# Gated SSD and S5 mixers on one Trainium2 core: scores and their products with the decays in PSUM, decay differences on ScalarE, y in one set of columns

## Chip, core and metric

The kernel runs on one core of a Trainium2 chip. The metric is the device time of one execution in microseconds. A core has TensorE (PE, matmuls; its weight loads are listed apart as PEld), VectorE (DVE), ScalarE (ACT), GpSimd (POOL) and SyncE (SP, which here issues transfers). Each engine works through its own list of instructions in order; a scheduler has fixed these lists when the kernel is built, and semaphores hold an engine back until what it needs is there.

## What is computed

One layer of a streaming encoder: 2048 positions and 16 learned meta tokens of width 1024, a gated SSD branch (16 heads of 64 in 4 groups, state 128) beside an S5 branch, and a squared-ReLU MLP. The change lies in the SSD branch alone. Its core in the reference:

```python
da_cs = jnp.cumsum(dt_c * a.reshape(g, r), axis=2)
seg = da_cs[:, :, :, None] - da_cs[:, :, None, :]
decay = jnp.exp(jnp.where(causal, seg, -jnp.inf))
scores = jnp.einsum("bclgn,bcsgn->bclsg", cc, bc)
y_diag = jnp.einsum("bclsg,bclsgr,bcsgrp->bclgrp", scores, decay, xdt)
states = jnp.einsum("bclgn,bclgr,bclgrp->bcgrpn", bc, decay_states, xdt)
...
y_off = jnp.einsum("bclgn,bcgrpn,bclgr->bclgrp", cc, h_prev, jnp.exp(da_cs))
return (y_diag + y_off).reshape(b, seq_len, n_heads, p)
```

The kernel takes chunks of 128 positions instead of 64, which gives the same function. So for each chunk and group of 4 heads there is one 128x128 matrix of scores, four 128x128 matrices of decays (one a head), their products, and y as the product of these with the inputs.

## The kernel before

The 2048 positions are worked through in four blocks (b = 0 to 3) of 512, each of four chunks (c) of 128. In a block, the groups g = 0 to 3 follow each other. For a group PE makes, as its main load, four units of the x/B/C projection (`xbc`, each followed by a convolution, `conv_tile`) and four units of the z and gate projection (`rhs_group`, evacuated by `evac_zg` at L1208 and L1209 into `zg`); each unit is 24 matmuls of 512 columns (in block 0, with the meta tokens, an `xbc` unit is 48 of 264). These matmuls write the banks `pd`, four in all, and a bank is free for the next unit when its evacuation has read it. Between the units `step()` puts the small work of the scan: with t counting the units of a group, t = 2 starts the decays (`Ssd.start`), t = 4 to 7 do `front(0)`, `front(1)`, `back(0)`, `front(2)`; `back(1)`, `front(3)`, `back(2)` and `back(3)` fall into t = 0 to 3 of the next group. The order in which an engine gets these instructions is the scheduler's, which shifts them further.

All matmul operands are split into a high and a low part, and `mm3` makes high x high, high x low and low x high, three matmuls into one result (L244, L245, L246).

What the change touches, for one chunk:

- `front(c)`: the inputs xs are transposed into the PSUM bank `sst` (L787) and scaled; `xhl` holds their high and low parts side by side. The scores go to the bank `psc` and are masked with the triangle `tri` into the SBUF tile `smask` (L837, VectorE). L839 multiplies the decays `csb` (SBUF, four heads) by it in place; ScalarE casts the result to its high part `mh` (L842), VectorE makes the low part `ml` (L843).
- `back(c)`: `pyo` is the part from the carried state, of which `hTh` (ScalarE, L811) and `hTl` are the parts. For each head L853 multiplies `mh` by both halves of `xhl` at once, 128 columns (high half and low half of the result stand side by side), and L855 adds `ml` times the high half on 64 columns. VectorE makes y from `pyo` (L861, four times) and adds both halves of `py` (L864, twice).
- `decays`: one DMA on SyncE's queue (L885) spreads the cumulated decays of a group over 128 partitions, 1 MB in SBUF (`csb`; one buffer in block 0, two in blocks 1 to 3). Then 16 VectorE instructions (L889, four chunks by four heads) subtract the column of cs and limit to zero, and one ScalarE instruction takes the exponential of all (L890).

Of the kernel before, what the change touches and what calls it, by code (L numbers as in the profile page):

```python
# [127 lines left out]
def _body(ctx, tc, d, out):  # L128
# [647 lines left out]
    class Ssd:  # L776
# [5 lines left out]

        def inputs(self, x, dts, i0, cs_, L):
            pl = self.pl
            pt = bank("sst")
            for i in range(2):
                T.transpose(pt[:L, i * P:(i + 1) * P], self.sd.xs[:, i, cs_], ident)  # L787
            x.pth = pt[:L, 0:256].rearrange("p (h q) -> p h q", h=4)
            x.xdt = pl.tile([P, 4, 64], F32, name="xdt", tag="xdt")
            xdd = pl.tile([P, 4, 64], F32, name="xdd", tag="xdd")  # L790
            V.tensor_tensor(x.xdt[:L], x.pth, h4(dts.dt, L, i0), op=ALU.mult)
            G.tensor_tensor(xdd[:L], x.xdt[:L], h4(dts.ds, L, i0), op=ALU.mult)
            x.xddh = pl.tile([P, 256], F32R, name="xddh", tag="xddh", bufs=2)
            x.xddl = pl.tile([P, 256], F32R, name="xddl", tag="xddl", bufs=2)
            xf = xdd.rearrange("p h q -> p (h q)")
            S.copy(x.xddh[:L], xf[:L])
            G.tensor_tensor(x.xddl[:L], xf[:L], x.xddh[:L].bitcast(F32), op=ALU.subtract)
# [14 lines left out]
            G.tensor_tensor(self.hl, f, self.hh.bitcast(F32), op=ALU.subtract)  # L812

        def start(self):
            self.dec = decays(self.pl, self.dts, self.g, self.b)

        def meta_in(self):
            self.mk = _K()
# [5 lines left out]
        def front(self, c):  # L824

            pl, sd, g, x = self.pl, self.sd, self.g, self.ck[c]
            x.cs_ = cs_ = slice(sd.t0 + c * P, sd.t0 + (c + 1) * P)
            self.inputs(x, self.dts, c * NH + g * 4, cs_, P)
            x.dx = pl.tile([P, 4, 64], F32, name="dx", tag="dx", bufs=2)
            V.tensor_tensor(x.dx, x.pth, drow[:, g * 4:g * 4 + 4].unsqueeze(2).broadcast_to([P, 4, 64]), op=ALU.mult)  # L830
            x.xhl = pl.tile([P, 4, 2, 64], F32R, name="xhl", tag="xhl", bufs=2)
            S.copy(x.xhl[:, :, 0, :], x.xdt)
            G.tensor_tensor(x.xhl[:, :, 1, :], x.xdt, x.xhl[:, :, 0, :].bitcast(F32), op=ALU.subtract)
            psc = bank("psc")
            mm3(psc[:, 0:P], sd.bh[:, cs_], sd.bl[:, cs_], sd.ch[:, cs_], sd.cl[:, cs_], True, True)
            sm = pl.tile([P, P], F32, name="smask", tag="smask", bufs=2)
            V.tensor_tensor(sm, psc[:, 0:P], tri, op=ALU.mult)  # L837
            csb = self.dec[:, c]
            V.tensor_tensor(csb, csb, sm.unsqueeze(1).broadcast_to([P, 4, P]), op=ALU.mult)  # L839
            x.mh = pl.tile([P, 4, P], F32R, name="mh", tag="mh", bufs=2)  # L840
            x.ml = pl.tile([P, 4, P], F32R, name="ml", tag="ml", bufs=2)
            S.copy(x.mh, csb)  # L842
            V.tensor_tensor(x.ml, csb, x.mh.bitcast(F32), op=ALU.subtract)  # L843

        def back(self, c):

            pl, sd, g, x, dts = self.pl, self.sd, self.g, self.ck[c], self.dts
            i0, cs_ = c * NH + g * 4, x.cs_
            py, po = bank("py"), bank("pyo")
            mm3(po[:, 0:256], sd.ch[:, cs_], sd.cl[:, cs_], self.hh, self.hl, True, True)  # L850
            pyv = py.rearrange("p (h a q) -> p h a q", h=4, a=2)
            for h in range(4):
                T.matmul(pyv[:, h].rearrange("p a q -> p (a q)"), x.mh[:, h, :],  # L853
                         x.xhl[:, h].rearrange("p a q -> p (a q)"), start=True, stop=False)
                T.matmul(pyv[:, h, 0, :], x.ml[:, h, :], x.xhl[:, h, 0, :], start=False, stop=True)  # L855
            self.update(x, sd.bth[:, c, :], sd.btl[:, c, :], dts.cd, i0, P)
            if c < NC4 - 1:
                self.split()
            x.y = y = pl.tile([P, 4, 64], F32, name="y_", tag="y_", bufs=2)
            for h in range(4):  # L860
                V.scalar_tensor_tensor(y[:, h, :], po[:, h * 64:h * 64 + 64], dts.E[:, i0 + h:i0 + h + 1],  # L861
                                       x.dx[:, h, :], op0=ALU.mult, op1=ALU.add)
            for a in range(2):
                V.tensor_tensor(y, y, pyv[:, :, a, :], op=ALU.add)  # L864

        def gate(self, c):

# [13 lines left out]
    def decays(pl, dts, g, b):  # L881

        t = pl.tile([P, NC4, 4, P], F32, name="csb", tag="csb", bufs=2 if b else 1)
        src = csd[b].rearrange("(c h) l -> c h l", h=NH)[:, g * 4:g * 4 + 4, :]
        nc.sync.dma_start(t, src.unsqueeze(0).broadcast_to([P, NC4, 4, P]))  # L885
        for c in range(NC4):
            for h in range(4):
                i = c * NH + g * 4 + h
                V.tensor_scalar(t[:, c, h, :], t[:, c, h, :], dts.cs[:, i:i + 1], 0.0, op0=ALU.subtract, op1=ALU.min)  # L889
        S.activation(t, t, AF.Exp)  # L890
        return t


    xp = pool("xn", stack=xp_st)
# [195 lines left out]
    for b in range(NB):  # L1090
# [22 lines left out]
        def step(mm):  # L1113

            n = step.n
            step.n += 1
            g, t = divmod(n, 8)
            with tc.issue_after(mm):
                if n == 0:
                    dts.turn()  # L1120
                    dts.sums()
                if g < NG:
                    x = ssd[g]
                    if t == 2:
                        x.start()
                    elif t == 4:
                        if b == 0:
                            x.meta_in()
                        x.front(0)
                    elif t == 5:  # L1130
                        if b == 0:
                            x.meta_out()
                        x.split()
                        x.front(1)
                    elif t == 6:
                        x.back(0)
                    elif t == 7:
                        x.front(2)
                        x.gate(0)
                if g > 0:  # L1140
                    x = ssd[g - 1]
                    if t == 0:
                        x.back(1)
                        x.gate(1)
                    elif t == 1:
                        x.front(3)
                    elif t == 2:
                        x.back(2)
                        x.gate(2)
                    elif t == 3:  # L1150
                        x.back(3)
                        x.gate(3)
                for f in later:
                    f()
                later.clear()
                if b == 0:
                    s5.step(n - 1)
                if n >= KSTART:
                    next(kept, None)
# [606 lines left out]
```

## Time and profile before

| | |
|---|---|
| median of 3 runs | 3305.94 us (3300.7 to 3306.1) |
| the profiled execution | 3306.5 us, its span 3304.8 us |
| mean granted clock of TensorE | 0.968 |
| busy: PE, DVE, POOL, ACT | 93%, 64%, 43%, 37% |
| mixers (blocks 0 to 3) | about 205 to 1860 us of the span |
| MLP | about 1860 to 3304 us |

The span runs from the first to the last instruction of the profiled execution; 1.7 us of its time lie around it. Times in rows are counted from the span's start. A row of idle time names the engine or transfer whose event ended the wait. Block 0 runs from about 205 to 730, block 1 to 1110, block 2 to 1465, block 3 to 1860; block 0 has the S5 scan of its own and its larger share of VectorE's work besides.

### The profile page before, as it was taken

The page shows a single profiled execution, that of the slowest core. Times are in us where ns is not written, and L with a number is a line of the kernel's source. Part 1 is how long each engine was busy: PE and PEld are TensorE (multiplying, and loading weights), DVE is VectorE, ACT ScalarE, POOL GpSimd, SP SyncE. Part 2 cuts the span into 40 slices and gives each one's busy share as a digit, 9 for nine tenths or more (in the row PEclk, how much of TensorE's full clock was granted, in tenths as well). Part 3 has the DMA queues.
Part 4 walks back from the last instruction along what each step waited for, and adds up shares of the span by engine and source line. Part 5 has one row for each costly group of instructions (what it writes and reads, how often), then busy time and mean ns, then how long its engine had stood idle before and what let it go on. Part 6 is the DMA issues. An engine that isn't in the chain of part 4 may idle for free. (4 is left out here: it accounts for less than half of the span.)

```text
span 3304.8 us, 50038 instructions
## 1 busy us (share of the span) xinstructions
PE 3083.7 (93%) x18353; PEld 2751.1 (83%) x18353; DVE 2105.5 (64%) x4298; ACT 1231.2 (37%) x2573; POOL 1428.1 (43%) x1736
## 2 busy tenths in 40 slices
PE   7899999998999999998999788998979999989998
PEld 6678888877888778876888688888979999989998
DVE  8969998426843576426854477767675555475555
ACT  6345554434432443334433343344442121142222
POOL 3346766523522344213433465665642222243443
PEclk9999999999999999999999889999989999999999
DMA  6477676775556654566756767777788888889998
GB/s 210 143 214 203 199 205 205 284 245 155 173 189 216 201 169 158 204 221 195 226 178 209 255 252 275 261 275 265 276 283 284 246 250 245 249 286 377 358 358 277
DMA packets 297877, 782.92 MB, mean 237 GB/s; under 512 B 90688, under 2 KB 132800, under 8 KB 268448
## 3 DMA queue, kind: packets, MB, share of 16 engines
q0 software_dynamic: 88832, 411.21, 37.4%
q1 hardware_dynamic: 206192, 367.29, 33.8%
q8 instruction: 146, 2.39, 0.3%
q10 hardware_dynamic: 2608, 1.22, 0.1%
q14 instruction: 99, 0.81, 0.1%
HBM read 563.66 MB, written 218.05 MB: 237 GB/s over the span
## 5 line engine op out<-in xcount | busy, mean ns | idle before, releaser
L1505 DVE TENSOR_TENSOR acc<-acc,p 128x512 f32<-128x512 f32 x330 | 225.7, 684 | 171.6 <-PE p L246 169.1
L244 PE MATMUL pd<-hnh,wc 128*128 128x384 f32 (+1 forms) x896 | 292.9, 328 | 34.9 <-DMA wc<-wcd 21.3
L244 PE MATMUL pd<-wu,xnh 128*128 128x512 f32 x768 | 309.8, 404 | 3.5 <-ACT cacc L750 3.0
L246 PE MATMUL pd<-wu,xnl 128*128 128x512 f32 x768 | 308.9, 402 | 0.0
L245 PE MATMUL pd<-wu,xnh 128*128 128x512 f32 x768 | 308.3, 401 | 0.0
L246 PE MATMUL pd<-hnh,wc 128*128 128x384 f32 (+1 forms) x896 | 291.6, 328 | 13.7 <-DVE wc L1346 10.5
L245 PE MATMUL pd<-hnl,wc 128*128 128x384 f32 (+1 forms) x896 | 291.8, 326 | 0.0
L228 POOL DMA_DIRECT2D wu<-wsd x168 | 96.0, 572 | 373.0 <-PE pd L246 305.6
L1356 POOL DMA_DIRECT2D wr<-wcd x227 | 122.3, 539 | 274.8 <-PE pd L246 138.7
L244 PE MATMUL pd<-xnh,wu 128*128 128x512 f32 (+1 forms) x640 | 232.8, 364 | 7.7 <-DMA wu<-wsd 6.5
L246 PE MATMUL pd<-xnh,wu 128*128 128x512 f32 (+1 forms) x640 | 229.3, 359 | 0.0
L245 PE MATMUL pd<-xnl,wu 128*128 128x512 f32 (+1 forms) x640 | 229.0, 358 | 0.0
L1356 POOL DMA_DIRECT2D wc<-wcd x221 | 118.3, 536 | 252.8 <-PE pd L246 136.8
L244 PEld LDWEIGHTS pd<-hnh,wc 128*128 128x128 f32 x896 | 173.6, 194 | 40.0 <-ACT hnh L994 13.5
L753 DVE SCALAR_TENSOR_TENSOR cacc<-craw,conv,cacc 128x512 f32<-128x512 f32 (+1 forms) x192 | 174.9, 912 | 24.5 <-ACT cacc L750 17.1
L246 PEld LDWEIGHTS pd<-hnh,wc 128*128 128x128 f32 x896 | 173.6, 194 | 19.9 <-DVE wc L1346 14.3
L244 PEld LDWEIGHTS pd<-wu,xnh 128*128 128x128 f32 x768 | 146.1, 190 | 35.4 <-ACT cacc L750 3.9
L245 PEld LDWEIGHTS pd<-hnl,wc 128*128 128x128 f32 x896 | 173.7, 194 | 0.0
L246 PEld LDWEIGHTS pd<-wu,xnl 128*128 128x128 f32 x768 | 146.3, 191 | 31.8 <-issue 0.2
L245 PEld LDWEIGHTS pd<-wu,xnh 128*128 128x128 f32 x768 | 146.0, 190 | 31.4 <-issue 0.2
L218 POOL TENSOR_TENSOR wu<-wst,wu 128x1024 fp32r<-128x1024 f32 x56 | 137.1, 2448 | 73.6 <-ACT wu L217 72.5
L244 PEld LDWEIGHTS pd<-xnh,wu 128*128 128x128 f32 x640 | 125.5, 196 | 24.9 <-issue 7.9
(1015 smaller groups left out, 9967.7 us busy)
## 6 DMA issues: line engine op xcount, KB each, us to landing
wu<-wsd POOLq DMA_DIRECT2D x168, 1024.0 KB, 5.3
wr<-wcd POOLq DMA_DIRECT2D x227, 512.0 KB, 5.1
wcd<-wc SPq DMA_DIRECT2D x224, 512.0 KB, 3.0
wc<-wcd POOLq DMA_DIRECT2D x221, 512.0 KB, 5.5
wsd<-wu SPq DMA_DIRECT2D x56, 1024.0 KB, 5.2
wst<-in_w SPq DMA_DIRECT2D x60, 512.0 KB, 5.8
csb<-csd SPq DMA_DIRECT2D x16, 1024.0 KB, 14.3
xt<-in_x SPq DMA_DIRECT2D x28, 512.0 KB, 3.8
```

The lines of the kernel that those rows point to most:

```text
L218: eng.tensor_tensor(t[:, 1], raw, t[:, 0].bitcast(F32), op=ALU.subtract)
L228: nc.gpsimd.dma_start(t, wsd[u - U_XBC])
L244: T.matmul(ps, lh, rh, start=first, stop=False, skip_group_check=open_)
L245: T.matmul(ps, lh, rl, start=False, stop=False, skip_group_check=open_)
L246: return T.matmul(ps, ll, rh, start=False, stop=last, skip_group_check=open_).ins
L753: V.scalar_tensor_tensor(acc[:, :n], raw[:, k:k + n], conv[:, mt, k:k + 1], acc[:, :n], op0=ALU.mult, op1=ALU.add)
L1356: nc.gpsimd.dma_start(t, wcd[di * 28 + j])
L1505: V.tensor_tensor(o, o, pv, op=ALU.add)
```

## The change

Three things are changed. First, the scores no longer have the bank `psc`: their matmuls write columns 256 to 383 of the bank `sst` that holds the transposed inputs, the mask is applied there in place, and the product with the decays is written to the bank `psc` instead of in place into `csb`; ScalarE's cast and VectorE's low part read it from there. Second, the differences in `decays` are made by ScalarE: 16 Relu instructions with scale -1 and cs as bias give the differences with the other sign, and the exponential takes scale -1. `decays` is now a generator in three pieces: the DMA is called at the end of t = 1, the first eight Relus in t = 2, the rest and the exponential in t = 3. Third, each head's y is made by `mm3` on one set of 64 columns, three matmuls instead of two, and VectorE adds `py` once.

```diff
@@ -782,7 +782,7 @@
 
         def inputs(self, x, dts, i0, cs_, L):
             pl = self.pl
-            pt = bank("sst")
+            x.pt = pt = bank("sst")
             for i in range(2):
                 T.transpose(pt[:L, i * P:(i + 1) * P], self.sd.xs[:, i, cs_], ident)
             x.pth = pt[:L, 0:256].rearrange("p (h q) -> p h q", h=4)
@@ -812,7 +812,8 @@
             G.tensor_tensor(self.hl, f, self.hh.bitcast(F32), op=ALU.subtract)
 
         def start(self):
-            self.dec = decays(self.pl, self.dts, self.g, self.b)
+            self.decs = decays(self.pl, self.dts, self.g, self.b)
+            self.dec = next(self.decs)
 
         def meta_in(self):
             self.mk = _K()
@@ -831,12 +832,11 @@
             x.xhl = pl.tile([P, 4, 2, 64], F32R, name="xhl", tag="xhl", bufs=2)
             S.copy(x.xhl[:, :, 0, :], x.xdt)
             G.tensor_tensor(x.xhl[:, :, 1, :], x.xdt, x.xhl[:, :, 0, :].bitcast(F32), op=ALU.subtract)
-            psc = bank("psc")
-            mm3(psc[:, 0:P], sd.bh[:, cs_], sd.bl[:, cs_], sd.ch[:, cs_], sd.cl[:, cs_], True, True)
-            sm = pl.tile([P, P], F32, name="smask", tag="smask", bufs=2)
-            V.tensor_tensor(sm, psc[:, 0:P], tri, op=ALU.mult)
-            csb = self.dec[:, c]
-            V.tensor_tensor(csb, csb, sm.unsqueeze(1).broadcast_to([P, 4, P]), op=ALU.mult)
+            sm = x.pt[:, 256:256 + P]
+            mm3(sm, sd.bh[:, cs_], sd.bl[:, cs_], sd.ch[:, cs_], sd.cl[:, cs_], True, True, True)
+            V.tensor_tensor(sm, sm, tri, op=ALU.mult)
+            csb = bank("psc").rearrange("p (h l) -> p h l", h=4)
+            V.tensor_tensor(csb, self.dec[:, c], sm.unsqueeze(1).broadcast_to([P, 4, P]), op=ALU.mult)
             x.mh = pl.tile([P, 4, P], F32R, name="mh", tag="mh", bufs=2)
             x.ml = pl.tile([P, 4, P], F32R, name="ml", tag="ml", bufs=2)
             S.copy(x.mh, csb)
@@ -848,11 +848,9 @@
             i0, cs_ = c * NH + g * 4, x.cs_
             py, po = bank("py"), bank("pyo")
             mm3(po[:, 0:256], sd.ch[:, cs_], sd.cl[:, cs_], self.hh, self.hl, True, True)
-            pyv = py.rearrange("p (h a q) -> p h a q", h=4, a=2)
+            pyv = py[:, 0:256].rearrange("p (h q) -> p h q", h=4)
             for h in range(4):
-                T.matmul(pyv[:, h].rearrange("p a q -> p (a q)"), x.mh[:, h, :],
-                         x.xhl[:, h].rearrange("p a q -> p (a q)"), start=True, stop=False)
-                T.matmul(pyv[:, h, 0, :], x.ml[:, h, :], x.xhl[:, h, 0, :], start=False, stop=True)
+                mm3(pyv[:, h], x.mh[:, h, :], x.ml[:, h, :], x.xhl[:, h, 0, :], x.xhl[:, h, 1, :], True, True)
             self.update(x, sd.bth[:, c, :], sd.btl[:, c, :], dts.cd, i0, P)
             if c < NC4 - 1:
                 self.split()
@@ -860,8 +858,7 @@
             for h in range(4):
                 V.scalar_tensor_tensor(y[:, h, :], po[:, h * 64:h * 64 + 64], dts.E[:, i0 + h:i0 + h + 1],
                                        x.dx[:, h, :], op0=ALU.mult, op1=ALU.add)
-            for a in range(2):
-                V.tensor_tensor(y, y, pyv[:, :, a, :], op=ALU.add)
+            V.tensor_tensor(y, y, pyv, op=ALU.add)
 
         def gate(self, c):
 
@@ -883,12 +880,15 @@
         t = pl.tile([P, NC4, 4, P], F32, name="csb", tag="csb", bufs=2 if b else 1)
         src = csd[b].rearrange("(c h) l -> c h l", h=NH)[:, g * 4:g * 4 + 4, :]
         nc.sync.dma_start(t, src.unsqueeze(0).broadcast_to([P, NC4, 4, P]))
+        yield t
         for c in range(NC4):
             for h in range(4):
                 i = c * NH + g * 4 + h
-                V.tensor_scalar(t[:, c, h, :], t[:, c, h, :], dts.cs[:, i:i + 1], 0.0, op0=ALU.subtract, op1=ALU.min)
-        S.activation(t, t, AF.Exp)
-        return t
+                S.activation(t[:, c, h, :], t[:, c, h, :], AF.Relu, bias=dts.cs[:, i:i + 1], scale=-1.0)
+            if c == 1:
+                yield
+        S.activation(t, t, AF.Exp, scale=-1.0)
+        yield
 
 
     xp = pool("xn", stack=xp_st)
@@ -1121,8 +1121,8 @@
                     dts.sums()
                 if g < NG:
                     x = ssd[g]
-                    if t == 2:
-                        x.start()
+                    if t in (2, 3):
+                        next(x.decs)
                     elif t == 4:
                         if b == 0:
                             x.meta_in()
@@ -1150,6 +1150,8 @@
                     elif t == 3:
                         x.back(3)
                         x.gate(3)
+                if t == 1 and g < NG:
+                    ssd[g].start()
                 for f in later:
                     f()
                 later.clear()
```

What the scheduler makes of it, at three places. First ScalarE in block 1, from the cast of group 0's last chunk (`mh`) to the first gate evacuation that follows the next exponential; `hTh` are the state casts of the two coming chunks, `csb_9047` and `csb_9050` are the decays of group 2. Before:

```order
L842 CAST mh_8437<-csb_7985 128x512 [waits DVE_49]
L811 CAST hTh_8518<-hT_101 128x256 [waits DVE_49,Activation_49]
L811 CAST hTh_8700<-hT_101 128x256 [waits PE_49,Activation_49]
L873 ACTIVATE dx_8269,yss_8530<-y__8522 128x256 [waits DVE_49]
L759 CAST ch_8298<-cacc_8565 128x512 [waits PE_49]
L890 ACT_TABLE_LOAD [waits DMAHW7_49,DVE_49]
L890 ACTIVATE csb_9047<-csb_9047 128x2048 [waits Activation_49]
L769 CAST bth_8300<-btp_8610 128x512 [waits PE_49]
L1208 ACT_TABLE_LOAD
L1208 ACTIVATE zg_8795<-pd_8617 128x256 [waits PE_49]
```

After:

```order
L842 CAST mh_8471<-psc_8469 128x512 [waits DVE_49,Activation_49]
L887 ACTIVATE csb_9050<-csb_9050,cs_7925 128x128 [waits DMAHW7_49]
L887 ACTIVATE csb_9050<-csb_9050,cs_7925 128x128 x15
L811 CAST hTh_8547<-hT_101 128x256 [waits DVE_49,Activation_49]
L811 CAST hTh_8739<-hT_101 128x256 [waits PE_49,Activation_49]
L870 ACTIVATE dx_8302,yss_8558<-y__8551 128x256 [waits DVE_49]
L749 COPY craw_9014<-pd_8989 128x512 [waits PE_49]
L890 ACT_TABLE_LOAD
L890 ACTIVATE csb_9050<-csb_9050 128x2048 [waits Activation_49]
L1210 ACT_TABLE_LOAD
L1210 ACTIVATE zg_8854<-pd_8659 128x256 [waits DVE_49]
```

The 16 Relus and their wait for the transfer (DMAHW) stand behind `mh` and ahead of both `hTh`; the evacuations of `zg` stand behind the exponential as before.

VectorE at the same place, before:

```order
L804 TENSOR_TENSOR hT_101<-hT_101,pS_8512 128x256 [waits PE_49]
L864 TENSOR_TENSOR y__8522<-y__8522,py_8499 128x256 [waits DVE_49] x2
L870 TENSOR_TENSOR y__8522<-y__8522,zg_8246 128x256 [waits DVE_49]
L874 TENSOR_SCALAR yss_8530<-yss_8530 128x1 [waits Activation_49]
L889 TENSOR_SCALAR csb_9047<-csb_9047,cs_7893 128x128 [waits DMAHW7_49]
L889 TENSOR_SCALAR csb_9047<-csb_9047,cs_7893 128x128 x15
L877 SCALAR_TENSOR_TENSOR y__8522<-y__8522,yrs_8533,nwssd_7820 128x256 [waits Pool_49]
L861 SCALAR_TENSOR_TENSOR y__8595<-pyo_8577,E_7894,dx_8425 128x64 [waits PE_49]
L861 SCALAR_TENSOR_TENSOR y__8595<-pyo_8577,E_7894,dx_8425 128x64 x3
```

After:

```order
L861 TENSOR_TENSOR y__8551<-y__8551,py_8524 128x256 [waits DVE_49,PE_49]
L804 TENSOR_TENSOR hT_101<-hT_101,pS_8541 128x256 [waits PE_49,Pool_49]
L867 TENSOR_TENSOR y__8551<-y__8551,zg_8279 128x256 [waits DVE_49]
L871 TENSOR_SCALAR yss_8558<-yss_8558 128x1 [waits Activation_49]
L874 SCALAR_TENSOR_TENSOR y__8551<-y__8551,yrs_8561,nwssd_7852 128x256 [waits Pool_49]
L875 SCALAR_TENSOR_TENSOR mixA_7832<-zg_8279,y__8551 128x256 [waits DVE_49]
L804 TENSOR_TENSOR hT_101<-hT_101,pS_8630 128x256 [waits PE_49]
L859 SCALAR_TENSOR_TENSOR y__8636<-pyo_8614,E_7926,dx_8460 128x64 [waits PE_49]
```

The 16 subtractions and their wait for the transfer are gone from this queue, and one addition of `py` (L864 before, L861 after) a chunk.

PE, the beginning of `back` for one chunk (group 0 of block 1, chunk 2): the part from the state and the y of two of the four heads. Before:

```order
L246 MATMUL pd_8619<-wu_8537,xnl_6989 128x512
L245 MATMUL pyo_8500<-hTl_8359,ch_7825 128x256 [waits Pool_49]
L246 MATMUL pyo_8500<-hTh_8358,cl_7826 128x256
L853 MATMUL py_8499<-xhl_8271,mh_8281 128x128 [waits DVE_49]
L855 MATMUL py_8499<-xhl_8271,ml_8282 128x64
L853 MATMUL py_8499<-xhl_8271,mh_8281 128x128
L855 MATMUL py_8499<-xhl_8271,ml_8282 128x64
```

After:

```order
L244 MATMUL pyo_8525<-hTh_8394,ch_7857 128x256 [waits PE_49]
L245 MATMUL pyo_8525<-hTl_8395,ch_7857 128x256 [waits Pool_49]
L246 MATMUL pyo_8525<-hTh_8394,cl_7858 128x256
L244 MATMUL py_8524<-xhl_8304,mh_8313 128x64 [waits PE_49]
L245 MATMUL py_8524<-xhl_8304,mh_8313 128x64
L246 MATMUL py_8524<-xhl_8304,ml_8314 128x64
L244 MATMUL py_8524<-xhl_8304,mh_8313 128x64
L245 MATMUL py_8524<-xhl_8304,mh_8313 128x64
L246 MATMUL py_8524<-xhl_8304,ml_8314 128x64
```

A head's two matmuls of 128 and 64 columns have become three of 64.

## Rows read from the trace of the kernel before

**Rows 1.** The page, busy us, share of the span and instructions of each engine.

```profile
PE 3083.7 (93%) x18353; PEld 2751.1 (83%) x18353; DVE 2105.5 (64%) x4298; ACT 1231.2 (37%) x2573; POOL 1428.1 (43%) x1736
```

**Rows 2.** Windows: stretch, us, PE, PEld, DVE, ACT, POOL busy, clock, DMA, GB/s.

```profile
205.00:490.00 285.00, 262.37 (x1635) 230.91 (x1636) 263.33 (x510) 147.12 (x327) 194.38 (x194) 0.94 0.73 206
490.00:730.00 240.00, 238.25 (x1168) 193.18 (x1167) 129.71 (x258) 106.06 (x211) 117.14 (x102) 1.00 0.71 241
...
1465.00:1860.00 395.00, 366.12 (x1789) 302.29 (x1788) 238.98 (x515) 161.69 (x310) 148.83 (x213) 0.97 0.62 203
```

**Rows 3.** VectorE's groups, 205 to 1860: form, count | busy, mean ns | idle before.

```profile
L839 DVE TENSOR_TENSOR csb<-csb,smask 128x512 f32<-128x512 f32 x64 | 75.4, 1184 | 1.1
L843 DVE TENSOR_TENSOR ml<-csb,mh 128x512 fp32r<-128x512 f32 x64 | 61.1, 959 | 14.4 <-ACT mh L842 14.3
L889 DVE TENSOR_SCALAR csb<-csb,cs 128x128 f32<-128x128 f32 x256 | 56.5, 296 | 79.0 <-DMA csb<-csd 79.0
...
L1301 DVE TENSOR_TENSOR xr<-xr,pd 128x512 f32<-128x512 f32 x31 | 21.2, 686 | 147.6 <-PE pd L246 86.2 <-DMA xr<-in_x 61.4
```

**Rows 4.** PE's groups, blocks 1 to 3 (730 to 1860), with the idle time before.

```profile
L853 PE MATMUL py<-xhl,mh 128*128 128x128 f32 x192 | 46.1, 291 | 16.4 <-ACT mh L842 16.4
...
L787 PE MATMUL sst<-ident,xs 128*128 128x128 f32 x96 | 20.3, 294 | 9.6 <-DVE y__11957 L861 3.2 <-DVE y__8595 L861 3.1 <-DVE y__9162 L861 2.3
...
L244 PE MATMUL psc<-ch,bh 128*128 128x128 f32 x48 | 14.4, 300 | 3.5 <-ACT ch L759 3.5
...
L244 PE MATMUL pd<-wu,xnh 128*128 128x512 f32 x558 | 224.4, 402 | 3.5 <-ACT cacc L750 3.0 <-DMA wu<-wsd 0.5
```

**Rows 5.** Timeline in block 1 (start, us, engine, line): SyncE, VectorE, PE.

```profile
790.97 0.36 SPq L885 DMA_DIRECT2D csb<-csd  x1
...
801.92 3.23 DVE L889 TENSOR_SCALAR csb<-csb,cs 128x128 f32<-128x128 f32 x16 [7.22 <-DMA csb<-csd]
...
806.46 0.66 PE L787 MATMUL sst<-ident,xs 128*128 128x128 f32 x2 [3.08 <-DVE y__8595 L861]
```

**Rows 6.** Windows behind two of PE's waits.

```profile
806.00:812.50 6.50, 6.04 (x20) 5.09 (x21) 4.01 (x12) 6.46 (x13) 0.41 (x1) 0.50 0.03 10
...
1518.00:1525.00 7.00, 6.95 (x24) 6.14 (x25) 6.39 (x12) 4.09 (x7) 3.34 (x5) 0.50 0.00 1
```

**Rows 7.** PE's timeline in block 1, wide and y matmuls.

```profile
786.55 0.40 PE L244 MATMUL pd<-wu,xnh 128*128 128x512 f32 x1
786.78 0.39 PE L245 MATMUL pd<-wu,xnh 128*128 128x512 f32 x1
...
788.43 0.30 PE L853 MATMUL py<-xhl,mh 128*128 128x128 f32 x1
788.57 0.24 PE L855 MATMUL py<-xhl,ml 128*128 128x64 f32 x1
...
789.10 0.36 PE L244 MATMUL pS<-xddh,bth 128*128 128x256 f32 x1
```

**Rows 8.** VectorE's timeline at the same place.

```profile
787.56 0.69 DVE L839 TENSOR_TENSOR csb<-csb,smask 128x512 f32<-128x512 f32 x1
...
790.25 0.68 DVE L843 TENSOR_TENSOR ml<-csb,mh 128x512 fp32r<-128x512 f32 x1
...
792.29 0.87 DVE L864 TENSOR_TENSOR y__8522<-y__8522,py 128x256 f32<-128x256 f32 x2
```

**Rows 9.** ScalarE's groups, 205 to 1860: a 128x128 form with a scale.

```profile
L277 ACT ACTIVATE xnh<-ntp,wmix 128x128 fp32r<-128x128 f32 x96 | 30.1, 367 | 12.2 <-DVE xnl L278 7.1 <-PE ntp L274 3.8
```

**Rows 10.** ScalarE's timeline around the site of rows 5.

```profile
792.46 0.71 ACT L811 CAST hTh<-hT 128x256 fp32r<-128x256 f32 x2 [3.56 <-DVE hT L804]
...
805.21 1.28 ACT L890 ACT_TABLE_LOAD   x1 [8.12 <-DVE csb L889]
806.51 1.91 ACT L890 ACTIVATE csb<-csb 128x2048 f32<-128x2048 f32 x1
...
810.20 0.38 ACT L1208 ACTIVATE zg<-pd 128x256 f32<-128x256 f32 x1
810.48 0.38 ACT L1209 ACTIVATE zg<-pd 128x256 f32<-128x256 f32 x1
```

## The prediction

> **What bounds the kernel now.** I read the engine totals first: TensorE (PE) is busy for 93% of the span, VectorE (DVE) 64%, GpSimd 43%, ScalarE (ACT) 37% [rows 1]. A mean over stages doesn't price an edit, so next the windows by stage [rows 2]. All edits lie in the mixers, 205 to 1860 us; the MLP behind them has none. Block 0 is special in its first half (205 to 490): PE is busy 262.37 of 285 us and DVE 263.33 of 285, so there both are near their limit. In the rest of block 0 PE is busy 99% and DVE 54%, and in block 3, the least full of blocks 1 to 3, 93% and 61%. So from 490 us on, work taken off VectorE is worth nothing by itself; only matmuls, and waits in which PE stands, count.
>
> Then the waits. VectorE idles 79.0 us in front of the subtractions for the transfer of the decays' rows [rows 3]. What reaches PE of that in blocks 1 to 3 is read from PE's own idle time [rows 4]: 16.4 us at the three block starts (py waits for mh), 9.6 us in mid-block, where the next chunk's transposes wait for y, and 6.5 us in small waits (3.5 of scores for a cast, 3.0 of a gate bank for the conv). Together 32.5 us. One of these sites in order of time [rows 5]: SyncE issues the 1 MB transfer at 790.97, VectorE stands 7.22 us and goes on at 801.92, which is 10.95 us after the issue; its sixteen subtractions take 3.23 us; the y sums behind them are late, and PE's next transposes have waited 3.08 us at 806.46. In the stretch behind that wait the granted clock is 0.50, the lower of the two levels, so 6.5 us there do the work of 3.25; behind the start of block 3 it is 0.50 again [rows 6]. I count five such stretches in blocks 1 to 3, 37.5 us in all, so about 19 us lost.
>
> **The change part by part.**
>
> *The y sum: more matmuls.* Before, a head took a 128-column and a 64-column matmul; now three of 64 columns. The columns streamed are the same (192 a head); the matmuls of a chunk grow from 8 to 12, over 64 chunks 256 more. What does one cost? In a back-to-back stretch the first of six y matmuls starts at 788.43 and what follows them at 789.10: 0.112 a matmul, of a mean width of 96 columns; two of 512 columns start 0.23 apart [rows 7], so five times the columns take twice the time. So narrow matmuls don't shrink with their columns: something that comes once per matmul, and every matmul has its own weight load (18353 of each [rows 1]), sets about 0.11. I take 0.11 for each of the 12: 4 x 0.112 = 0.45 us a chunk, 28.7 us for 64 chunks, 21.5 of it in blocks 1 to 3 where PE is full. Bounds: 0 if only columns count; 0.14, the step from 788.43 to 788.57, for all twelve gives 12 x 0.14 - 8 x 0.112 = 0.78 a chunk, 50 us. I take 0.112, a mean over just these operands.
> The Trainium skill ("TensorE: Matmul & The Clock Gate", LDWEIGHTS) gives a weight load of P columns about P/1.2 ns, which makes an estimated 107 ns for the 128 columns here, however few are streamed behind it. The trace's 0.11 agrees. That rule speaks against this edit: by it the four extra loads of a chunk are paid in full, while by streamed columns alone they would cost nothing.
>
> *VectorE's relief.* Gone are 256 subtractions (56.5 us [rows 3], and the wait in front of them) and 64 of the y additions (two take 0.87 [rows 8], so 0.43 each: 28 us). The product with the decays reads its scores from PSUM and writes PSUM, and the low part reads PSUM: their means are 1184 and 959 ns with both operands in SBUF, and a 128x512 addition with one operand in PSUM takes 686 [rows 3]. If both come to 0.69, that is 32 + 17 us. Bounds: no gain, as no row here shows VectorE writing PSUM, and the 49 us. In all up to 133 us, some 7.6 us in each quarter (one group of heads) of blocks' time. From 490 us on it is worth nothing by the windows above. In the first half of block 0, PE idles 23 us and about 0.06 of the clock is missing (17 us): of those 40 I let the relief win back 20. Bounds 0 and 40.
> The Trainium skill ("SBUF — State Buffer", SBUF: two separate sides) says that a VectorE instruction with two SBUF inputs and a GpSimd instruction shut each other out of a shared pair of ports. The trace agrees as far as the same product took 0.69 once [rows 8] and 1184 ns in the mean; by the rule the full 49 us would come, and the sum goes by its own bounds.
>
> *ScalarE gets the subtractions, and with them the wait.* 256 Relus of 128x128. VectorE's took 3.23/16 = 0.20 each; ScalarE's 128x128 form with a scale takes 0.367 [rows 9], part of which overlaps its neighbour. I take the middle, 0.28: 4.5 us a group, 72 us in all. As work that is nothing: ACT is busy for 41 to 52% of the windows in rows 2. What matters is that the engine is in order: the Relus wait for the transfer, and behind them stand things that PE needs soon.
> Look at group 0 to 1 of block 1 (the ScalarE order in the section on the change). The buffer of group 2 comes free with the last product of group 0, and the transfer goes out then; the Relus stand right behind mh of that chunk. Behind them stand hTh (needed by the very next chunk's matmuls), two casts, Exp, and the gate evacuations that give PE its banks back. Before, ScalarE had done hTh in 0.71 us at 792.46, and only Exp and evacuations were behind the wait [rows 10].
> Replay with the rows' durations, zero at the end of that product: the transfer is ready at 10.95, Relus 4.5, hTh 0.7: 16.2. PE has in the new order, between those scores and the matmul on hTh, 29 matmuls of 512 columns (6.8 us), 6 of 256 (0.7), 12 of y (1.35), less 1.5 us for mask and product: 7.3. So PE stands 8.9 us. Then the evacuation is late: casts 1.2, table load 1.28, Exp 1.91, table load 1.28, two evacuations of 0.33 [rows 10] end at about 22.5, where PE has had 2.6 us more of work since 16.2 and one weight unit's remainder: about 2 more. Sum 10.7. The same count at the other five mid-block sites gives 9.1, 6, 7, 4 and 5, with more wide matmuls in between: 42 us, in place of the 16.1 (9.6 + 6.5) of before: +26. Two things help already in this count: the product no longer writes the SBUF buffer, so the transfer goes at its end and not after the low part, about 2.7 us sooner (787.56 + 0.69 against 790.25 + 0.68 [rows 8]), and the transfer is issued a step earlier in the program. Against it, the scheduler has put the product itself later in PE's stream, one unit of 24 matmuls (5.6 us) or more.
> At block starts Exp of group 0 now stands behind the wait for group 1's transfer on ScalarE; on the other hand the first y has moved 61 wide matmuls (14 us) down PE's stream. Replayed: 7.8, 0 and 6.7 us for the three starts, 14.5 against 16.4: -2.
> Clock: a stretch of half clock behind each longer wait, at 3.3 us lost each; eight of them (six mid-block, two starts) are 26 us, against 19 before: +7.
> Block 0 has one buffer for the decays, so there ScalarE waits for a whole transfer in each group, behind the product of the last chunk: I put 3 us of it on PE for each of four groups: +12 (bounds 0, since VectorE waited at the same place before, and 36 by the 8.9 above).
>
> *The sum*: 28.7 (matmuls) - 20 (relief) + 12 (ScalarE's wait, block 0) - 2 (starts) + 26 (mid-block) + 7 (clock) = +51.7. The profiled execution took 3306.5 us (span 3304.8); its sum is 3358, and the median of runs lies 0.6 lower: **3357 us**.
>
> **The rivals.**
> *Faster: the wait leaves PE's path.* The transfer goes out a step earlier, and the Relus need no VectorE. If ScalarE finds the rows there, the waits at starts and in mid-block end (16.4 + 9.6 = 26), the clock behind them comes back (16 of 19), block 0 gains 12 net of its matmuls: 28.7 - 26 - 16 - 12 = -25: 3281. For it: 79 us of waits in before, and DVE at 92% in block 0's first half. Against: the order of after still issues at the product of the last chunk, and rows 5 show 10.95 us for a transfer, which PE's 7.3 us do not cover. It decides if fewer than about 4 us are left at a site. Chance 0.25.
> *The same: one wait for another.* ScalarE's wait costs PE what VectorE's did, relief in block 0 (30) pays for the matmuls: 3306. Chance 0.12, half of it within the bound. If columns alone set the price of the y matmuls, my forecast falls by 28.7 to 3329, still slower; in the rival above it gives 3252.
> *Much slower.* The evacuation of gate banks makes every site cost some 17 us, blocks 1 to 3 lose 102 - 16 + 10 of clock, block 0 the 36 of its bound less 20: 28.7 + 96 + 16 = +141 at worst, half of that being likelier: 3400 to 3447. For it: the wait stands in front of four kinds of ScalarE work. Against: before's stall behind 10.95 us of transfer was 3 us. Chance 0.13.
>
> **How the numbers follow.** Forecast 0.50, with a range of its own of 3325 to 3395 (relief 0 to 40, matmuls 0 to 50, mid-block sites 16 to 60). Faster 0.25, same 0.12, much slower 0.13. To leave out 2 in 10: 0.10 of the faster rival lies under 3278, 0.10 over 3405: range 3278 to 3405. A measurement tells 0.2%, 6.6 us, from no change: faster 0.27 (0.25 and some of the same-rival), within 0.10, slower 0.63.
>
> **What would show it.** In the trace of after: starts of y matmuls 0.11 apart in sets of twelve (or 0.06 to 0.08, and the first term is gone); the product of the decays at 0.69; ScalarE waiting on the transfer at L887 in some 13 places of 3 to 10 us, and PE waiting there for hTh and zg; PE busy in 205 to 490 above 262 us. I am wrong if L887 waits little, or if hTh and the gate banks are not what PE then waits for, or if block 0 shortens by far more than 20 us.

## The result

| | before | after |
|---|---|---|
| median | 3306.02 us | 3424.39 us |
| lowest and highest of 4 runs | 3300.7 to 3310.1 | 3421.7 to 3427.3 |
| span of the profiled execution | 3304.8 us | 3420.1 us |

The ratio is 1.036, 95% interval 1.0342 to 1.0378: 118 us slower. The forecast was slower by 51 us, with a range up to 3405. The sign was right; two thirds of the loss came from a part that the forecast had booked as a gain.

The page of after, its first part, answers [rows 1]:

```profile
PE 3150.9 (92%) x18609; PEld 2801.8 (82%) x18609; DVE 1993.1 (58%) x3978; ACT 1298.0 (38%) x2829; POOL 1395.1 (41%) x1736
```

256 matmuls more, VectorE relieved by 112 us, ScalarE loaded by 67. The MLP is as it was; the loss is in the mixers. Windows of after, cut at the first matmul of each block's dt product (us, then busy time of PE, PEld, DVE, ACT, POOL, granted clock, DMA share, GB/s):

```profile
175.00:702.00 527.00, 490.06 (x2791) 423.12 (x2790) 354.63 (x674) 265.07 (x592) 299.25 (x287) 0.92 0.69 209
702.00:1112.00 410.00, 381.93 (x1835) 312.23 (x1833) 185.05 (x412) 162.08 (x365) 121.54 (x202) 0.97 0.53 177
1112.00:1520.00 408.00, 382.60 (x1832) 313.04 (x1831) 185.03 (x412) 157.84 (x361) 115.95 (x202) 0.97 0.52 173
1520.00:1975.00 455.00, 418.61 (x1995) 340.24 (x1994) 217.02 (x442) 181.28 (x386) 146.85 (x221) 0.96 0.59 196
```

The same cuts in the kernel before (other edges than [rows 2]):

```profile
174.00:668.00 494.00, 464.88 (x2722) 398.86 (x2721) 388.40 (x754) 247.90 (x528) 307.53 (x287) 0.96 0.73 222
668.00:1050.00 382.00, 368.00 (x1769) 302.34 (x1768) 207.15 (x492) 142.66 (x299) 131.19 (x202) 0.98 0.57 190
1050.00:1425.00 375.00, 366.81 (x1772) 301.24 (x1771) 208.72 (x492) 141.77 (x297) 125.77 (x202) 0.99 0.56 190
1425.00:1854.00 429.00, 400.32 (x1932) 327.78 (x1931) 242.74 (x522) 167.82 (x324) 153.19 (x221) 0.97 0.63 207
```

So the blocks lost 33, 28, 33 and 26: all alike, although only block 0 has a VectorE that is near its limit. From the gaps between matmuls and the records of the clock I sum over the four blocks: PE idle 127 us against 80 (+47), time at half clock 174 against 85 (+89, half of it lost: 44), and 28.6 us of additional matmul time (below). Together 120, and the blocks' own times differ by 120.

What PE waits for in after, 200 to 2000 us (total, times, longest); before had none of the first three, and [rows 4] shows what it had instead:

```profile
PE pd L244 <- ACT zg L1211: 19.4, 11, 7.3
PE pyo L244 <- ACT hTh L811: 16.9, 6, 8.0
PE sst L244 <- DVE dx L831: 16.4, 8, 4.4
PE pd L244 <- DMA wu<-wsd: 15.4, 11, 4.2
PE pd L244 <- ACT cacc L750: 7.8, 4, 5.9
```

The second line is the forecast's wait. At its site in block 1:

```profile
847.94 4.78 ACT L887 ACTIVATE csb<-csb,cs 128x128 f32<-128x128 f32 x16 [9.28 <-DMA csb<-csd]
852.62 0.69 ACT L811 CAST hTh<-hT 128x256 fp32r<-128x256 f32 x2
...
853.06 0.58 PE L244 MATMUL pyo<-hTh,ch 128*128 128x256 f32 x1 [7.96 <-ACT hTh L811]
```

The third is one that the forecast does not contain: the scores (`sst<-ch,bh`) wait for VectorE's read of the transposed inputs (`dx`), which stand in the same bank. Two chunks' fronts in after (group 1 of block 1), PE and VectorE in order of time:

```profile
857.92 0.63 PE L787 MATMUL sst<-ident,xs 128*128 128x128 f32 x2
...
860.83 0.41 DVE L831 TENSOR_TENSOR dx<-sst,drow 128x256 f32<-128x256 f32 x1
...
866.25 0.22 PE L244 MATMUL sst<-ch,bh 128*128 128x128 f32 x1
...
869.59 0.69 DVE L839 TENSOR_TENSOR psc<-csb,sst 128x512 f32<-128x512 f32 x1
...
870.93 0.69 DVE L843 TENSOR_TENSOR ml<-psc,mh 128x512 fp32r<-128x512 f32 x1
...
872.80 0.38 PE L787 MATMUL sst<-ident,xs 128*128 128x128 f32 x2
```

And in the kernel before, the same two chunks:

```profile
808.19 0.31 PE L244 MATMUL psc<-ch,bh 128*128 128x128 f32 x1
...
810.11 0.63 PE L787 MATMUL sst<-ident,xs 128*128 128x128 f32 x2
810.39 0.46 PE L244 MATMUL psc<-ch,bh 128*128 128x128 f32 x1
...
812.24 0.42 DVE L830 TENSOR_TENSOR dx<-sst,drow 128x256 f32<-128x256 f32 x1
...
814.31 1.23 DVE L839 TENSOR_TENSOR csb<-csb,smask 128x512 f32<-128x512 f32 x1
```

Before, PE starts the transposes and scores of both chunks within 4.4 us (806.46 [rows 5] to 810.86) and VectorE follows. In after the scores come 8.3 us behind the transposes, as PE puts a unit of wide matmuls between, and the second chunk starts only when the first chunk's low part is made: 14.9 us apart instead of 3.7. Over the whole trace, all 64 chunks of after start their scores when VectorE's `dx` has ended; before, 8 of 64 did. Shown in the rows is the order; that it costs the time is for the experiments.

### The profile page after: what moved, and what is told of

It is laid out like the page before. It is cut to its first block, busy times and chain, and to the rows that moved or that the text cites. A ratio compares the mean times of both kernels' runs of the same rounds, so it can differ in the third digit from the quotient of the medians.

```text
span 3420.1 us, 50570 instructions
## 1 busy us (share of the span) xinstructions
PE 3150.9 (92%) x18609; PEld 2801.8 (82%) x18609; DVE 1993.1 (58%) x3978; ACT 1298.0 (38%) x2829; POOL 1395.1 (41%) x1736
## 5 line engine op out<-in xcount | busy, mean ns | idle before, releaser
L244 PE MATMUL pd<-xnh,wu 128*128 128x512 f32 (+1 forms) x640 | 237.0, 371 | 29.5 <-ACT zg L1211 17.6
L246 PE MATMUL pd<-xnh,wu 128*128 128x512 f32 (+1 forms) x640 | 232.4, 364 | 0.0
```

Source lines behind the costliest of these rows:

```text
L244: T.matmul(ps, lh, rh, start=first, stop=False, skip_group_check=open_)
L246: return T.matmul(ps, ll, rh, start=False, stop=last, skip_group_check=open_).ins
```

## The experiments

Each is compared with the kernel before on the same chip; figures in us are differences of medians. Theory W is the forecast's (ScalarE's wait for the decays), N says the narrow matmuls cost more than their time, B that the banks are at fault; B was refined on the way. A new order of instructions is drawn for every variant, so a few us each way say nothing.

**One part at a time.** e1 takes the third part of the diff alone into the kernel before, e2 the second, e3 the first; e4 is the changed kernel with the y sum (third part) put back.

> The kernel before, with the y sum alone in one set of columns (twelve matmuls of 64 columns a chunk instead of eight of 128 and 64; one addition of py less). Theory W (the loss behind the matmuls comes from ScalarE's wait for the decays' transfer): the 0.45 us a chunk alone, +29 us, 3335. Theory B (it comes from the banks: scores share the bank of the transposed inputs, the product holds a bank): the same +29. Theory N (the narrow matmuls bring the granted clock down, so the edit costs more than its matmuls): +60 to +100, 3366 to 3406, with more time at half clock than before.

Measured: 3325.53, ratio 1.0081 (1.0066 to 1.0096), +25. As expected without N; N falls.

> The kernel before, with the decays' differences alone on ScalarE (16 Relus a group, in the three pieces of the changed kernel). Theory W: most of the rest, +50 to +90 us, 3356 to 3396, PE waiting for hTh, zg and cacc behind L887's wait. Theory B and theory N: within 10 us of before.

Measured: 3311.28, 1.0028 (1.0015 to 1.0041), +10. W falls as the main cause.

> The kernel before, with the scores in the bank of the transposed inputs and the product with the decays in PSUM alone. Theory W: no loss, 0 to -20 us (VectorE's product and low part at 0.69). Theory B: most of the rest, +50 to +90, PE waiting at the scores for VectorE's dx (L831). Theory N: no loss.

Measured: 3400.87, 1.0301 (1.0279 to 1.0323), +100. The part on which the forecast had put a gain makes, alone, nearly as much as the whole loss.

> The changed kernel with the y sum as before (128 and 64 columns, two additions of py). Theory W and theory B: 29 us less than the changed kernel, 3395. Theory N: 60 to 100 less, 3325 to 3365.

Measured: 3399.28, 1.0302 (1.0287 to 1.0318), +98: 20 less than the changed kernel. The parts do not add up: alone they cost 25, 10 and 100, which is 135, and together 118.

In e3 PE's wait at the scores is the largest of all in the mixers (total, times, longest):

```profile
PE sst L244 <- DVE dx L830: 29.2, 14, 7.4
```

Over the four blocks of e3 PE idles 48 us more than before, and stands 99 us longer at half clock, of which half is lost: 97 together, and its blocks are 98 longer.

**Taking that part to pieces**, all on the kernel before.

```diff
-            psc = bank("psc")
-            mm3(psc[:, 0:P], ...)                     # e5: scores in the shared bank,
+            psc = x.pt[:, 256:256 + P]                # mask and product in SBUF
+            mm3(psc, ..., True)
```

> The kernel before; the scores alone move to columns 256 to 383 of the bank of the transposed inputs. Mask to SBUF and product in SBUF as before. Theory B1 (the shared bank: the scores stand behind VectorE's reads of the transposes, xdt and dx, so a chunk's chain crosses PE, VectorE, PE, VectorE): most of the 100 us of e3_psum_alone, +60 to +110, 3361 to 3411. Theory B2 (the product holds a PSUM bank until the low part is made, of four that the small work shares): within 15 us of before. Theory B3 (both in equal parts): +50.

Measured: 3308.97, 1.0026 (1.0015 to 1.0037), +8. The same wait is there, and small:

```profile
PE sst L244 <- DVE dx L830: 4.3, 7, 1.2
```

```diff
+            sm = bank("scr")[:, 0:P]                  # e6: a bank of their own,
+            mm3(sm, ...)                              # mask there in place
+            V.tensor_tensor(sm, sm, tri, op=ALU.mult)
+            csb = bank("psc")...                      # product in another bank
```

> The kernel before; scores in a bank of their own, masked there in place, and the product with the decays written to another PSUM bank. B1: no loss, rather a gain by VectorE's faster product and low part, -20 to +10. B2: +60 to +110, as one bank more than before is held. B3: +50.

Measured: 3300.9, 1.0001 (0.9986 to 1.0015), 0. Neither half of the part costs much, +8 and 0; B1 and B2 fall both as they stood, and so does B3.

> The kernel before; scores in their own bank, masked there in place, the product read from there and written in place to SBUF as before. No theory gives a loss: the bank is held about one product longer (0.7 to 2 us). VectorE's product comes to 0.69 from 1.18: -20 to 0 us.

Measured: 3294.17, 0.9979 (0.9964 to 0.9993), -7. (e6 with the product in place in `csb`.)

```diff
+            x.pt = bank("sst")                        # e8: e3, scores ahead of
+            mm3(x.pt[:, 256:256 + P], ..., True)      # the transposes
             self.inputs(x, ...)
```

> As e3_psum_alone, but the scores are put into the shared bank ahead of the transposes, so that they wait for no VectorE read. B1: most of the 100 us comes back, 3300 to 3335, unless the transposes now wait for the scores' operands. B2: no change against e3_psum_alone, about 3400.

Measured: 3310.9, 1.0027 (1.0016 to 1.0039), +10. Same banks, same holding to the end of the product, 90 us less than e3: with the product in PSUM, what matters is that the scores stand behind VectorE.

**Banks or the wait?**

```diff
-            V.tensor_tensor(sm, sm, tri, op=ALU.mult)
+            V.tensor_tensor(sk, sm, tri, op=ALU.mult) # e9: e3, mask to SBUF
```

> As e3_psum_alone (3401), but the mask writes SBUF, so the shared bank is free after the mask and not after the product; the product still goes to a PSUM bank held until the low part. Theory R (a ring of four banks: a bank held longer, by a chain that has the trip over PE in it, holds up the next users of that slot, state update and S5 among them; both holds are needed): in between, 3320 to 3370. If it is the shared bank's hold through mask and product alone: 3300 to 3320. If it is the product's bank alone: 3385 to 3405.

Measured: 3407.76, 1.0313 (1.0292 to 1.0333), +103. Theory R and the shared bank's hold fall; it comes nearest to the range for the product's bank, which alone cost nothing in e6. e9 differs from e5 (+8) only in where the product goes.

```diff
-            py, po = bank("py"), bank("pyo")
+            py = bank("py")                           # e10: on the changed kernel
+            po = py[:, 256:512]
```

> The changed kernel (3424), with py and pyo (256 columns each) in one bank instead of two, so that a chunk takes one bank less of the ring of four; all else, the trip scores-after-transposes included, is as in the changed kernel. Theory R: a good part comes back, 40 to 90 us, 3334 to 3384. If the trip over PE itself is the cause (no bank involved): no change, 3410 to 3430, or slower by the shared bank.

Measured: 3416.34, 1.0342 (1.0319 to 1.0364), +111: some 8 better than the changed kernel. Theory R, too few banks, falls in both.

> The changed kernel with the scores in a bank of their own again (mask there in place, product in PSUM as in the changed kernel): the trip is gone, the ring has one user more. By e6_product_psum (no loss) most comes back: 3330 to 3350, which is the kernel before plus 29 for the y matmuls plus 10 for the decays. If the changed kernel's loss is the holding of banks alone, nothing comes back.

Measured: 3346.75, 1.0129 (1.0112 to 1.0147), +42, as expected: the changed kernel with e6's two lines for the scores.

**The wait itself.** Theory S: the wait lengthens a chunk's front, with the product in PSUM the fronts no longer overlap, and the whole chain of small work falls behind the wide matmuls. Its sign is on ScalarE: gate evacuations that find no free buffer, since the gate of the group before has not ended. In e3 (total, times, longest; before has none of these):

```profile
ACT zg L1207 <- DVE mixA L877: 30.8, 15, 4.2
```

An instance in e3; PE's line is where it arrives:

```profile
907.22 0.38 ACT L1207 ACTIVATE zg<-pd 128x256 f32<-128x256 f32 x1 [2.58 <-DVE mixA L877]
...
907.93 0.80 PE L244 MATMUL pd<-xnh,wu 128*128 128x512 f32 x1 [2.25 <-ACT zg L1208]
```

Little of PE's idle time is seen to come this way: in e3 all its waits for gate banks are 13.2 us. In after they are 19.4, but ahead of 17.5 of these ScalarE had been busy, with 0.06 us of idle time or less, ever since its wait for the decays' transfer. The longest:

```profile
1322.08 4.78 ACT L887 ACTIVATE csb<-csb,cs 128x128 f32<-128x128 f32 x16 [6.84 <-DMA csb<-csd]
1326.77 0.36 ACT L1210 ACTIVATE zg<-pd 128x256 f32<-128x256 f32 x1
...
1327.44 0.79 PE L244 MATMUL pd<-xnh,wu 128*128 128x512 f32 x1 [7.27 <-ACT zg L1211]
```

So the gate waits are a sign that the small work lags; that the loss runs through them is not shown.

e14 moves the scores in the changed kernel as e8 does. e15 makes e6 wait without sharing a bank:

```diff
             scr = bank("scr")
+            V.tensor_copy(scr[:, P:P + 1], x.dx[:, 3, 63:64])   # e15, e16
             sm = scr[:, 0:P]
```

> The changed kernel with one line moved: the scores go into the shared bank ahead of the transposes, so that they wait for no VectorE read; banks and all else as in the changed kernel. Theory S: as with a bank of their own, 3335 to 3355 (before + 29 for the y matmuls + 5 to 15). If holding the shared bank longer is what costs: 3400 to 3424.

Measured: 3337.29, 1.0108 (1.0091 to 1.0125), +35. The scores' matmuls, moved ahead, take 83 us off; +35 is e1 and e2 together.

> e6_product_psum (3301: scores in a bank of their own, product in PSUM) with one VectorE copy of one column into the scores' bank, behind dx, so that the scores must wait for VectorE although they share no bank with the transposes. The copy itself is 64 x 0.06 us on an engine with room. Theory S: the loss of e3_psum_alone comes back, +60 to +110, 3360 to 3410, with ScalarE's waits of zg for mixA. If sharing the bank is what costs: within 15 us of 3301.

Measured: 3382.61, 1.0245 (1.0229 to 1.026), +80. A copy of one column (0.157 us in the mean of the trace, 10 us of VectorE in all, more than was expected of it), and most of the loss is back, with PE where it was in e3:

```profile
PE scr L244 <- DVE scr L835: 35.9, 18, 7.5
```

> e7_mask_psum (3294: scores in a bank of their own, masked in place, product back in SBUF) with the copy of e15 that makes the scores wait for VectorE. e15 lost 80 with the product in PSUM. If the wait costs only together with the product in PSUM (e5_shared_bank lost 8 with the wait alone): 3295 to 3315, and fronts of two chunks overlap (the next transposes start before the low part of the first chunk ends). If the wait costs by itself and e5 was spared by its smaller number of banks: 3340 to 3390.

Measured: 3313.94, 1.0043 (1.0029 to 1.0058), +16, in the first range, and the fronts overlap (table below). Against e7 the wait costs 23, so it is not free with the product in SBUF either.

> The changed kernel (3424) with five instead of four gate buffers (zg) in blocks 1 to 3; block 0 as it is. Theory S (scores behind VectorE lengthen a chunk's front, the fronts of two chunks follow each other serially, the gate of a group ends so late that the next group's gate evacuation finds no buffer, and PE no bank): some of the 66 us that blocks 1 to 3 lose beyond the matmuls come back, 15 to 45, 3379 to 3409, and ScalarE's waits of zg for mixA get fewer there. If the small work is simply too slow, a fifth buffer fills up as well: 0 to -8, 3416 to 3424.

Measured: 3445.99, 1.0438 (1.0422 to 1.0453), +144: 25 slower than the changed kernel. ScalarE's waits stay:

```profile
ACT zg L1210 <- DVE mixA L875: 33.5, 17, 3.7
```

So this expectation of S was wrong: with a fifth buffer the waits stay. Missing buffers show the lag and do not make it. Why the kernel got slower still is open.

> The changed kernel (3424) with the decays' differences back on VectorE, all at t = 2 as before. By the forecast's price for that part (12 - 2 + 26 + 7 = 43): 3381. By e2_decays_alone (+10): 3414. If the late chunk chain already covers ScalarE's wait: 3420 to 3430, no change.

Measured: 3392.73, 1.0266 (1.023 to 1.0301), +87: taking the decays' part out of the changed kernel is worth 31, where alone it cost 10.

**For a faster kernel.** e12 is e6 in blocks 1 to 3 and e7 in block 0; e17 is e8 with the product back in `csb`.

> The kernel before with e6_product_psum's product (PSUM) in blocks 1 to 3 and e7_mask_psum's (SBUF) in block 0. By the blocks of those two (e6 takes some 20 us off blocks 1 to 3, e7 3 us off block 0): 3278 to 3285. If the blocks' gains are the luck of one schedule: 3290 to 3310.

Measured: 3291.77, 0.9955 (0.9939 to 0.9971), -13: the lowest ratio, though its interval overlaps those of e7 and e17. Half of the 23 that the blocks had promised is there; block 3 of e6 was partly the luck of its order (its 417 us became 428).

> The kernel before with scores first in the shared bank, masked there in place, and the product back in SBUF: no wait of the scores for VectorE, one bank less a chunk, VectorE's product at 0.69 us. A candidate for a faster kernel: 3280 to 3300. If the transposes are late because they now follow the scores: 3300 to 3315.

Measured: 3291.06, 0.9972 (0.9955 to 0.9989), -7, as expected.

**What they say together.** Four combinations, with the loss or gain of each kernel:

| | product in SBUF | product in PSUM |
|---|---|---|
| scores free of VectorE | 0 (before), -7 (e7), -7 (e17) | 0 (e6), +10 (e8) |
| scores behind VectorE | +8 (e5), +16 (e16) | +100 (e3), +103 (e9), +80 (e15) |

From the timelines I took the time of a group, from the first transposes of chunk 0 to the last gate instruction (`mixA`) of chunk 3. The first two rows are means over the 12 groups of blocks 1 to 3, the third is the median over all 16 groups:

| | before | e5 | e16 | e6 | e14 | e3 | e15 | after |
|---|---|---|---|---|---|---|---|---|
| a group, us | 62 | 64 | 64 | 60 | 58 | 71 | 70 | 74 |
| a front, transposes to low part, us | 10.7 | 14.9 | 14.6 | 9.4 | 7.8 | 11.9 | 12.2 | 11.8 |
| chunk 1's transposes, behind chunk 0's low part, us | -5.7 | -10.8 | -6.6 | 0.1 | 1.8 | -0.2 | -0.7 | 0.0 |

With the product in SBUF the fronts overlap (third row below zero), and a long front does little harm (e5, e16). With the product in PSUM they mostly follow each other (the first group of blocks 1 to 3 still overlaps), and a short front does no harm (e6, e14). Long and in sequence makes a group 8 to 12 us longer, and this is the combination of the changed kernel. Shown: for the large loss both conditions are needed, and the wait, not the shared bank as such, is one of them (whether sharing makes the 20 us between e15 and e3 is open). Not settled: why the order has no overlap once the product is in PSUM, and by which waits the longer groups reach PE beyond those at the scores. One bank less a chunk (e10) brought little back, which speaks against a plain lack of banks; the order that the scheduler draws may have other reasons, and none was tried.

## Why the prediction was wrong, step by step

**The y matmuls: right.** Twelve of them in after, the first, the last, and what follows:

```profile
841.40 0.19 PE L244 MATMUL py<-xhl,mh 128*128 128x64 f32 x1
...
842.55 0.28 PE L246 MATMUL py<-xhl,ml 128*128 128x64 f32 x1
842.66 0.36 PE L244 MATMUL pS<-xddh,bth 128*128 128x256 f32 x1
```

1.26 us a chunk; eight took 0.81 (median of the stretches like [rows 7]); 0.45 more, 28.6 for 64 chunks, forecast 28.7. Alone (e1) the edit costs 25. That 64 columns cost as much as 128 agrees with the Trainium skill ("TensorE: Matmul & The Clock Gate", LDWEIGHTS), by which the load goes with the weights' columns.

**VectorE's relief: the durations right, the worth wrong.** Product and low part, 205 to 1900 us, against 1184 and 959 ns in [rows 3]:

```profile
L839 DVE TENSOR_TENSOR psc<-csb,sst 128x512 f32<-128x512 f32 x64 | 44.4, 693 | 54.3 <-ACT csb L890 52.7
L843 DVE TENSOR_TENSOR ml<-psc,mh 128x512 fp32r<-128x512 f32 x64 | 44.1, 689 | 30.8 <-ACT mh L842 30.6
```

That is the upper bound of the step (31 + 17 us). I let it win 20 in block 0; where the faster product stands without the wait (e6, e7) it wins 0 and 7 in the whole kernel, and block 0 of e6 was even 9 slower.

**The step that failed: the scores' new place was costed at nothing.** The part "VectorE's relief" counted what the product reads and writes, and left out that the scores now share a bank with tiles that VectorE reads; the sum has no term for it. Of the order of after I read ScalarE and y only, and not the scores. Their wait for VectorE, together with the product in PSUM, is worth 83 us in the changed kernel (e14). The Trainium skill ("PSUM — Partial Sum Buffer", PSUM bank collisions raise a hardware error) has the rule that speaks against the edit: accesses of two engines are to be kept apart by bank and quadrant of partitions, or simply by bank, and not by address. The order agrees: scores in columns 256 to 383 wait for reads of columns 0 to 255, and in e15 for a copy into column 128.

**ScalarE's wait: the mechanism right, the size too large.** The first site stood 7.96 us where the replay gave 8.9, and 16 Relus took 4.78 us (forecast 4.5). But the step's terms, 12 - 2 + 26 + 7 = 43, were measured as 10 alone (e2) and 31 inside the changed kernel (e18). What the forecast named as its signs is there: L887 waits for the transfer 16 times, 79.1 us in all, and directly behind these waits PE stands for `hTh` and gate banks, 25 us in blocks 1 to 3 and 5 in block 0; the replay had 42 and 14.5, and 12. Alone, such waits fall partly into time that PE lost anyway: in e2 PE waits 12.0 us for gate banks, but at `py` for `mh` only 5.5 in place of the 16.4 of [rows 4].

**The rivals.** "Much slower" named 3400 to 3447 and holds the time, but by luck: late evacuations behind ScalarE's wait are there, but the decays' part is worth 31 us in the changed kernel, not the 112 that the rival adds to the matmuls. Its chance of 0.13 was too small since every rival was built on the decays' transfer: the spread covered one mechanism's size, not a second mechanism. Three slips of the working change nothing in this: half of 141 is 70, which gives 3376 and not 3400 for that rival; the faster rival counts block 0's matmuls twice, in 28.7 and in "12 net", and with 21.5 comes to 3274; and 133 us of relief are 8.3 a group of heads, not 7.6.

## To carry to other kernels

In these kernels, putting an operand into a bank that another engine still reads added a wait even though the columns differ; ask of every move within PSUM which engine now has to be done first, and put the producer that needs nobody ahead of the one that is read. Cost a part by the chain it lengthens, not by the engine it relieves: two edits of 0 and 8 us made 100 together, as with one the neighbouring chains no longer overlapped and the other made each chain longer. When waits for a buffer appear, one buffer more tells in one run whether the lack of a buffer is the cause.

## Not expected of the hardware

A small loss in idle time came with a larger loss in clock: in block 0 PE idled 8 us more (37 against 29), but stood at half clock for 82 us instead of 38, which is 22 us of work. In this stretch of after PE is busy 83%, with three waits of 1.9 to 3.1 us, at a mean clock of 0.59:

```profile
569.00:606.00 37.00, 30.74 (x137) 27.30 (x138) 26.91 (x69) 14.15 (x34) 15.68 (x20) 0.59 0.32 76
```
